# Summing the four partial sums of an adaLN gate on VectorE instead of through a copy and a 0/1 product

## The chip, the cores and the metric

The kernel runs on one core of a Trainium2 chip. The metric is the device time of one execution in microseconds, taken as the median over several runs; lower is better.

## The reference

One layer of a hybrid decoder is computed for a prompt of 1024 tokens and for 8 samples of 4 tokens each. The whole working is float32. What matters here is the condition path: nine condition rows (one of the prompt, eight of the samples) go through one linear layer whose last third is the gate of the residual.

```python
def adaln_in(x, c, w_ada, b_ada, g_norm):
    mod = jax.nn.silu(c) @ w_ada + b_ada
    shift, scale, gate = jnp.split(mod, 3, axis=-1)
    h = rmsnorm(x, g_norm) * (1 + scale[:, None, :]) + shift[:, None, :]
    return h, gate[:, None, :]

def layer(x, c, ...):
    h, gate = adaln_in(x, c, w_ada, b_ada, g_norm)
    (mq, mk, mv, mi, mf, mo, mz, aq, ak, av, az, gm, ga) = split_in(h @ w_in)
    ...
    u = jax.nn.sigmoid(gm) * (y_m @ w_mo) + jax.nn.sigmoid(ga) * (y_a @ w_ao)
    x = x + gate * (u @ w_o)
```

`c` has 9 rows of 1024, `w_ada` is 1024 x 3072, so the gate is 9 x 1024. The kernel works it out as two halves of 512 columns (`ga0`, `ga1`).

## The kernel before, in words

The program is one long run of projections on TensorE, with everything else laid beside them. After the norm and the shift and scale of the conditions (up to about 65 us) the input projections follow column block by column block: the attention's queries (`g_aq`), then the mLSTM's queries, keys and values head by head (`g_mq`, `g_mk`, `g_mv`; three pieces of 384, 384 and 288 columns each, float32 split into a high and a low part, hence three products for each), then the blocked products of the gates (`bx`, `bw`, `by`, `bz`), the output projections (`g_w_mo`), and the last rows (`foX`, `foW`, `foY`, `foZ`).

Side work is fed in between these products. It is written as Python generators, and a planner, `class Side`, decides while the program is being built where each next step of a generator stands in TensorE's order. The planner keeps a clock of its own, `now`, which each product moves on by its assumed cost (`mm`, line 254). A step says `yield lag, banks`: the next step comes at the earliest `lag` later, only at a visit (at least 1.5 after the last one that issued products) and only when the PSUM bank class that it names is free by the planner's account (`HOLD`, line 109). Streams run side by side: `a` the attention units (`unit`, line 813: loads `uqv`, `ukv`; scores `sc`; the softmax on VectorE and ScalarE; transposes `pt`; `oT`), `m` the mLSTM heads (`head`, line 1024: loads `hq`, `hk`, `hv`, `et`, `qw`; `tk`, `tv`, `S`; `U`; `n`; `ty`), `x` the sums of blocks (`sum_blocks`, line 1292, tiles `hb`), `g` the gate that is changed here.

TensorE's order is therefore written out by the planner (`in_order`, line 206). VectorE and ScalarE are tied to the program's order only before line 1892 and in the last rows; in between a scheduler orders them when the program is built, and then each engine runs its list in order. SyncE issues most of the loads and stores, in one list too. PSUM has eight banks in four classes of two; `pb` (line 187) hands out class `b`, which `pt`, `tk`, `tv`, `ty` and the gate share.

The gate itself is `ada_gate` (line 1896). For each half `j` it loads eight tiles of `w_ada` (`adar_ga`) and the bias (`gb`, nine partitions), and then runs `ada_rows` (line 346): eight products with 32 columns of weights each, of which four stand side by side in the array and write to the partitions from 0, 32, 64 and 96 of one bank, `ada_ga`. Each of these four quarters then holds a partial sum over two of the eight tiles; rows 0 to 8 of a quarter are the nine conditions. ScalarE copies the bank to `adas_ga`, and a step later a product with the constant `s9`, which has a one in row r, r+32, r+64, r+96 of column r, adds the four quarters (`gp`, 9 x 512). VectorE adds the bias, multiplies by 0.25, and five DMAs store the half (`gbD`, `gsD`); it is read again only when the output weights are prepared, some 130 us later. After the second half, `c32` is loaded anew.

Of the kernel before, what the change touches and what calls it, by code (L numbers as in the profile page):

```python
# [15 lines left out]
ALU = mybir.AluOpType  # L16
# [19 lines left out]
C_ID, C_S9, C_TRI, C_CM, C_AM, C_TS, C_CS, C_RS, C_S32, C_BM, C_S64 = 0, 128, 137, 265, 393, 649, 681, 713, 745, 777, 785  # L36
# [136 lines left out]
def body(tc, a):  # L173
    nc = tc.nc
    with ExitStack() as ctx:
# [5 lines left out]
        def pg(shape, name):  # L181
            return ps.tile(shape, F32, tag="g", bufs=2, name=name)

        def pa(shape, name):
            return ps.tile(shape, F32, tag="a", bufs=2, name=name)

        def pb(shape, name):
            return ps.tile(shape, F32, tag="b", bufs=2, name=name)

        def po(shape, name):  # L190
            return ps.tile(shape, F32, tag="o", bufs=2, name=name)

        def ht(shape, name, dt=F32):
            return sp.tile(shape, dt, tag="half", bufs=43, name=name)
# [11 lines left out]
        def in_order(ins, eng="PE"):  # L206
            i = getattr(ins, "ins", ins)
            no_sync(i, [last[eng]] if eng in last else [])
            last[eng] = i
# [15 lines left out]
        V, S, G = Ordered(nc.vector, "V"), Ordered(nc.scalar, "S"), Ordered(nc.gpsimd, "G")  # L225
# [15 lines left out]
        def dma(out, in_, late=False):  # L241
            stores(in_.tensor)
            issue(out, in_, late)
# [10 lines left out]
        def mm(out, lhsT, rhs, start, stop, share=1, more=False):  # L254
            n = int(np.prod(rhs.shape[1:]))
            side.now += max(n, 250) / 2400 if rhs.dtype == F32R else max(n * 4 // share, 128) / 2400
            side.products += 1
            in_order(nc.tensor.matmul(out, lhsT, rhs, start=start, stop=stop, skip_group_check=more))  # L258
# [48 lines left out]
        cst = cp.tile([128, C_END], F32, name="cst")  # L307
# [35 lines left out]
                dma(raws[-1], a["w_ada"][chunk, :, k])  # L343
            return raws

        def ada_rows(raws, name, mS):
            acc = pb([128, 512], f"ada_{name}")
            for k0 in (0, 4):
                for k in range(k0, k0 + 4):
                    j = 32 * (k % 4)  # L350
                    mm(acc[j:j + 32], c32[:, k], raws[k], start=(k < 4), stop=(k >= 4), share=4)
                yield 2.0, ("b" if k0 == 0 else "")
            S.copy(mS, acc)
            yield 2.5, "b"

        def ada_chunk(raws, name, done):
            mS = ht([128, 512], f"adas_{name}")
            yield from ada_rows(raws, name, mS)
            tp = pb([128, 4, 9], f"adat_{name}")
            for j in range(4):  # L360
                mm(tp[:, j], mS[:, j * 128:(j + 1) * 128], cst[:, C_S9:C_S9 + 9], start=True, stop=True)
            done(tp)
# [1458 lines left out]
        for n in order[:2]:  # L1821
# [5 lines left out]
        acc = [(pg([128, 384], "g_ak0"), po([128, 384], "g_av0")),  # L1827
               (po([128, 384], "g_ak1"), pg([128, 384], "g_av1")),
               (pa([128, 384], "g_ak2"), pa([128, 384], "g_av2"))]
        for q, kk in enumerate(two):  # L1830
# [44 lines left out]
            else:  # L1875
                pair_end(1, acc[1])
                gp = pb([128, 9, 8], "gp")
# [16 lines left out]
        gbD, gsD = dp.tile([1, D], F32, name="gbD"), dp.tile([NS, D], F32, name="gsD")  # L1894

        def ada_gate():
            s9 = cst[:, C_S9:C_S9 + 9]
            for j in range(2):
                cj = slice(j * 512, (j + 1) * 512)
                raws = []  # L1900
                for k in range(KT):
                    raws.append(ht([128, 512], f"adar_ga{j}{k}"))
                    dma(raws[-1], a["w_ada"][4 + j, :, k])
                    yield 2.0, ""
                gb = ht([128, 512], f"gb{j}")[:9]
                dma(gb, a["b_gate"][:, cj].to_broadcast((9, 512)))
                yield 5.0, "b"
                mS = ht([128, 512], f"adas_ga{j}")
                yield from ada_rows(raws, f"ga{j}", mS)
                yield 1.5, "b"  # L1910
                gp = pb([128, 512], f"gp{j}")[:9]
                mm(gp, s9, mS, start=True, stop=True)
                V.tensor_tensor(gb, gp, gb, op=ALU.add)
                V.tensor_scalar(gb, gb, 0.25, None, op0=ALU.mult)
                dma(gbD[:, cj], gb[0:1])
                for t in range(NT):
                    dma(gsD.rearrange("(b t) e -> b t e", t=NT)[:, t, cj], gb[1:9])
                yield 3.0, "b" if j == 0 else ""
            dma(c32, hD[:, :, SEQ:T])
# [64 lines left out]
        for g in range(4):  # L1984
            queries(g)
        side.add("g", ada_gate())
        side.add("s", sample_attention(), "b")
        blocks["t1"] = block(0, 1)
# [340 lines left out]
```

## Time and profile before

| what | us |
|---|---|
| median of 3 runs (845.09, 845.72, 845.74) | 845.72 |
| profiled execution, first to last instruction | 843.1 |
| TensorE (PE) busy in it | 823.9 |
| VectorE (DVE) busy | 599.2 |
| ScalarE (ACT) busy | 416.0 |

The profiled execution has no device time of its own on record; its span is 2.6 us shorter than the median of the runs, and that much is taken to lie around the span. PE and PEld are the products and the weight loads of TensorE, DVE is VectorE, ACT ScalarE, POOL GpSimd, SP SyncE; a row `L258` is line 258, the helper through which all products go. A float32 product shows as two records in the trace.

### The profile page before, as it was taken

The page shows a single profiled execution, that of the slowest core. Times are in us where ns is not written, and L with a number is a line of the kernel's source. Part 1 is how long each engine was busy: PE and PEld are TensorE (multiplying, and loading weights), DVE is VectorE, ACT ScalarE, POOL GpSimd, SP SyncE. Part 2 cuts the span into 40 slices and gives each one's busy share as a digit, 9 for nine tenths or more (in the row PEclk, how much of TensorE's full clock was granted, in tenths as well). Part 3 has the DMA queues.
Part 4 walks back from the last instruction along what each step waited for, and adds up shares of the span by engine and source line. Part 5 has one row for each costly group of instructions (what it writes and reads, how often), then busy time and mean ns, then how long its engine had stood idle before and what let it go on. Part 6 is the DMA issues. An engine that isn't in the chain of part 4 may idle for free.

```text
span 843.1 us, 15367 instructions
## 1 busy us (share of the span) xinstructions
PE 823.9 (98%) x5185; PEld 680.6 (81%) x5185; DVE 599.2 (71%) x1601; ACT 416.0 (49%) x1027; POOL 63.3 (8%) x108
## 2 busy tenths in 40 slices
PE   6999999999999999999999999999999999999996
PEld 3779999879989878888878777777777779997775
DVE  4887884556667586655766875788878998865676
ACT  5663346655655454554543534444436554334343
POOL 0120000000110000000000000000002104250000
PEclk9999999999999999999999999999999999999998
DMA  9996548337745653454656584556446586634522
GB/s 332 371 358 200 146 150 297 119 111 237 247 133 177 193 163 103 162 175 153 206 185 207 194 253 127 178 151 152 127 126 211 190 266 212 215 95 168 200 106 107
DMA packets 117859, 158.18 MB, mean 188 GB/s; under 512 B 29056, under 2 KB 64512, under 8 KB 117748
## 3 DMA queue, kind: packets, MB, share of 16 engines
q1 hardware_dynamic: 111556, 146.44, 55.1%
q10 hardware_dynamic: 4752, 6.56, 2.1%
q0 software_dynamic: 1472, 4.20, 1.3%
q8 instruction: 41, 0.67, 0.3%
q14 instruction: 38, 0.31, 0.1%
HBM read 113.41 MB, written 44.75 MB: 188 GB/s over the span
## 4 chain that ended last, share of the span: by engine, by line
PE 93%; DVE 4%; DMA 1%; issue 1%; ACT 1%; SPq 0%; DVEq 0%; ACTq 0%
PE by L258 10%; PE bx L258 10%; PE bw L258 10%; PE g_aq L258 6%; PE g_w_mo L258 6%; PE bz L258 5%; PE g_mk L258 4%; PE g_mq L258 4%; PE g_mv L258 3%; PE foW L258 3%; PE foX L258 3%; PE foY L258 2%; PE sc L258 2%; PE oT L258 2%; PE foZ L258 2%; PE smp L258 2%
## 5 line engine op out<-in xcount | busy, mean ns | idle before, releaser
L219 ACT ACTIVATE p<-p,nmx 128x256 f32<-128x256 f32 (+1 forms) x64 | 31.0, 486 | 26.6 <-DVE nmx L219 22.3
L258 PE MATMUL g_aq<-h_h,wh_aq 128*128 128x384 f32 (+1 forms) x96 | 32.4, 337 | 0.0
L258 PE MATMUL g_w_mo<-ym_l,wh_w_mo 128*128 128x384 f32 (+1 forms) x96 | 31.1, 324 | 0.0
L258 PE MATMUL g_aq<-h_l,wh_aq 128*128 128x384 f32 (+1 forms) x96 | 31.0, 323 | 0.0
L258 PE MATMUL g_w_mo<-ym_l,wl_w_mo 128*128 128x384 f32 (+1 forms) x96 | 31.0, 323 | 0.0
L258 PE MATMUL g_aq<-h_h,wl_aq 128*128 128x384 f32 (+1 forms) x96 | 31.0, 323 | 0.0
L258 PE MATMUL g_w_mo<-ym_h,wh_w_mo 128*128 128x384 f32 (+1 forms) x96 | 31.0, 323 | 0.0
L219 DVE CUSTOM_DVE_ANT_0 p<-sc,cst,sink 128x256 f32<-128x256 f32 (+1 forms) x64 | 26.1, 463 | 3.6 <-PE sc L258 3.5
L258 PE MATMUL g_mk<-h_h,wh_mk 128*128 128x384 f32 (+1 forms) x72 | 24.8, 344 | 0.0
L258 PE MATMUL g_mq<-h_h,wh_mq 128*128 128x384 f32 (+1 forms) x72 | 24.4, 339 | 0.0
L219 DVE TENSOR_TENSOR et<-et,cst 128x384 f32<-128x384 f32 (+1 forms) x12 | 6.2, 513 | 24.9 <-DMA et<-nmd 24.9
L219 ACT ACTIVATE gt<-gt 128x512 f32<-128x512 f32 (+1 forms) x17 | 10.4, 613 | 26.9 <-DVE gt L219 26.2
L258 PE MATMUL g_mk<-h_l,wh_mk 128*128 128x384 f32 (+1 forms) x72 | 23.3, 323 | 0.0
L258 PE MATMUL g_mq<-h_l,wh_mq 128*128 128x384 f32 (+1 forms) x72 | 23.3, 323 | 0.0
L258 PE MATMUL g_mk<-h_h,wl_mk 128*128 128x384 f32 (+1 forms) x72 | 23.2, 323 | 0.0
L258 PE MATMUL g_mq<-h_h,wl_mq 128*128 128x384 f32 (+1 forms) x72 | 23.2, 323 | 0.0
L219 ACT ACTIVATE et<-et,an 128x128 f32<-128x128 f32 x32 | 11.2, 394 | 23.1 <-DVE et L219 17.8
L258 PEld LDWEIGHTS g_aq<-h_h,wh_aq 128*128 128x128 f32 x96 | 18.0, 188 | 1.4 <-issue 1.2
L246 POOL DMA_DIRECT2D oD<-uqv x16 | 8.8, 553 | 134.1 <-ACT uqv L219 130.8
L219 ACT ACTIVATE p<-p,den 128x256 f32<-128x256 f32 (+1 forms) x32 | 14.7, 490 | 8.1 <-DVE den L219 7.9
L258 PEld LDWEIGHTS g_w_mo<-ym_h,wh_w_mo 128*128 128x128 f32 x96 | 18.0, 188 | 0.0
L258 PEld LDWEIGHTS g_w_mo<-ym_l,wh_w_mo 128*128 128x128 f32 x96 | 18.0, 188 | 0.0
(1969 smaller groups left out, 2851.8 us busy)
## 6 DMA issues: line engine op xcount, KB each, us to landing
hb<-hD SPq DMA_DIRECT2D x24, 256.0 KB
x<-xT SPq DMA_DIRECT2D x16, 256.0 KB
early_h<-w_ada SPq DMA_DIRECT2D x8, 512.0 KB
adar_ga<-w_ada SPq DMA_DIRECT2D x16, 256.0 KB
wr_ga<-w SPq DMA_DIRECT2D x16, 256.0 KB
wr_gm<-w SPq DMA_DIRECT2D x16, 256.0 KB
taD<-gt SPq DMA_DIRECT2D x16, 256.0 KB
tmD<-gt SPq DMA_DIRECT2D x16, 256.0 KB
```

The costliest lines, as they stand in the source:

```text
L219: ins = f(*args, **kw)
L246: ins = (eng or nc.sync).dma_start(out, in_)
L258: in_order(nc.tensor.matmul(out, lhsT, rhs, start=start, stop=stop, skip_group_check=more))
```

## The change

The copy to `adas_ga` and the product with `s9` go, and so do the two steps of the planner between them. Instead VectorE adds the four quarters of the bank one after another to the bias tile, straight from PSUM: four additions of 9 x 512 for each half, where there was one. `ada_rows` is cut in two, so that the other user of it (the shift and scale in the first 65 us) keeps its copy.

```diff
-        def ada_rows(raws, name, mS):
-            acc = pb([128, 512], f"ada_{name}")
+        def ada_products(raws, acc):
             for k0 in (0, 4):
                 for k in range(k0, k0 + 4):
                     j = 32 * (k % 4)
                     mm(acc[j:j + 32], c32[:, k], raws[k], start=(k < 4), stop=(k >= 4), share=4)
                 yield 2.0, ("b" if k0 == 0 else "")
+
+        def ada_rows(raws, name, mS):
+            acc = pb([128, 512], f"ada_{name}")
+            yield from ada_products(raws, acc)
             S.copy(mS, acc)
             yield 2.5, "b"
...
                 yield 5.0, "b"
-                mS = ht([128, 512], f"adas_ga{j}")
-                yield from ada_rows(raws, f"ga{j}", mS)
-                yield 1.5, "b"
-                gp = pb([128, 512], f"gp{j}")[:9]
-                mm(gp, s9, mS, start=True, stop=True)
-                V.tensor_tensor(gb, gp, gb, op=ALU.add)
+                acc = pb([128, 512], f"ada_ga{j}")
+                yield from ada_products(raws, acc)
+                for r in range(0, 128, 32):
+                    V.tensor_tensor(gb, acc[r:r + 9], gb, op=ALU.add)
                 V.tensor_scalar(gb, gb, 0.25, None, op0=ALU.mult)
```

More of the change, by code (lines that the diff above doesn't have):

```diff
@@ L1896, in ada_gate @@
         def ada_gate():
-            s9 = cst[:, C_S9:C_S9 + 9]
             for j in range(2):
```

## The prediction

> **What bounds the kernel now.** I read the page first, then busy time by stretches, then TensorE's waits, then the gate's own instructions, and last the order of the changed program's instructions, which holds no times.
>
> ```profile
> span 843.1 us, 15367 instructions
> PE 823.9 (98%) x5185; PEld 680.6 (81%) x5185; DVE 599.2 (71%) x1601; ACT 416.0 (49%) x1027; POOL 63.3 (8%) x108
> PE 93%; DVE 4%; DMA 1%; issue 1%; ACT 1%; SPq 0%; DVEq 0%; ACTq 0%
> ```
>
> TensorE's products fill the span and make up nearly all of the chain that ended last. By stretches (columns: stretch, total, then busy time of PE, PEld, DVE, ACT, POOL):
>
> ```profile
> 60.00:280.00 220.00, 219.99 (x1672) 195.16 (x1665) 141.18 (x503) 115.26 (x350) 13.39 (x29) 1.00 0.58 180
> 280.00:430.00 150.00, 146.53 (x914) 121.14 (x914) 98.30 (x297) 76.52 (x201) 5.93 (x17) 1.00 0.56 173
> ```
>
> From 60 to 280 us, where both halves of the gate lie, TensorE has 0.01 us of idle time; from 280 to 430 it has 3.47, and its waits there are these four (us in total, times, longest):
>
> ```profile
> PE bx L258 <- ACT gt L219: 1.2, 1, 1.2
> PE smp L258 <- ACT hv L219: 1.0, 1, 1.0
> PE by L258 <- DVE mkv L219: 0.9, 1, 0.9
> PE n L258 <- DVE C L219: 0.5, 1, 0.5
> ```
>
> So an instruction taken off TensorE in the first stretch shortens the kernel by its place in TensorE's order, unless another engine then comes late.
>
> **What is removed.** The gate's product and copy, and the VectorE work behind them:
>
> ```profile
> L258 PE MATMUL gp<-adas_ga,cst x4: 592/595/598, 183.6 to 256.6; 128*9 128x512 f32 x4
> L219 ACT COPY adas_ga<-ada_ga x2: 567/567/567, 162.0 to 251.6; 128x512 f32<-128x512 f32 x2
> L219 DVE TENSOR_TENSOR gb<-gp,gb x2: 678/678/678, 184.7 to 257.2; 9x512 f32<-9x512 f32 x2
> ```
>
> The durations of products overlap, so I price them by the starts around them:
>
> ```profile
> 182.59 0.44 PE L258 MATMUL oT<-p,ukv 128*64 128x128 f32 x4
> ...
> 183.61 1.03 PE L258 MATMUL gp<-adas_ga,cst 128*9 128x512 f32 x2
> 184.57 0.44 PE L258 MATMUL g_mq<-h_h,wh_mq 128*128 128x384 f32 x1
> 184.85 0.34 PE L258 MATMUL g_mq<-h_l,wh_mq 128*128 128x384 f32 x1
> 185.02 0.34 PE L258 MATMUL g_mq<-h_h,wl_mq 128*128 128x384 f32 x1
> ...
> 255.83 0.29 PE L258 MATMUL g_mq<-h_l,wh_mq 128*128 128x288 f32 x1
> 255.96 0.29 PE L258 MATMUL g_mq<-h_h,wl_mq 128*128 128x288 f32 x1
> 256.19 1.03 PE L258 MATMUL gp<-adas_ga,cst 128*9 128x512 f32 x2
> 257.14 0.40 PE L258 MATMUL g_mq<-h_h,wh_mq 128*128 128x288 f32 x1
> 257.38 0.29 PE L258 MATMUL g_mq<-h_l,wh_mq 128*128 128x288 f32 x1
> ```
>
> First half: 183.61 to 184.57, 0.96 us; the detour out of the projection stays, because `oT` stands there anyway. Second half: 0.95 us, and the detour goes with it. Neighbours of 288 columns start 0.13 apart (255.83 to 255.96), but 0.23 pass before `gp` and 0.24 after the first product behind it, so the way out and back costs 0.10 + 0.11 = 0.21. Together 0.96 + 0.95 + 0.21 = **2.12 us off TensorE**. ScalarE loses two copies, 1.1 us; it is half idle, and I count nothing for that.
>
> **What is added.** Three more additions on VectorE for each half, from partitions 32, 64 and 96 of PSUM onto partition 0. The trace does not show that on nine partitions; it does show the same move on 32, in the sums of the last sample rows:
>
> ```profile
> L219 DVE TENSOR_TENSOR fo8s<-fo,fo8s x6: 682/685/692, 785.1 to 809.4; 32x512 f32<-32x512 f32 x6
> L219 DVE TENSOR_TENSOR wor<-wor,gb x16: 683/686/694, 401.8 to 493.0; 128x512 f32<-128x512 f32 x16
> 257.25 0.68 DVE L219 TENSOR_TENSOR gb<-gp,gb 9x512 f32<-9x512 f32 x1 [0.64 <-PE gp L258]
> 257.96 0.42 DVE L219 TENSOR_SCALAR gb<-gb 9x512 f32<-9x512 f32 x1
> ```
>
> Bounds are 0.68 and 0.69 us; I take 0.68, the row with nine partitions. A step that needs the one before starts 0.71 after it (257.25 to 257.96), so four take 2.84 us, 2.13 more than now, 4.3 us for both halves.
>
> [...]
>
> **Is it covered in the first half?** The order up to the first gate is unchanged, so its surroundings can be read from the trace of before:
>
> ```profile
> 159.17 1.06 PE L258 MATMUL ada_ga<-adar_ga,c 128*32 128x512 f32 x8
> 159.79 0.69 DVE L219 TENSOR_TENSOR wl_mq<-wr_mq,wh_mq 128x512 fp32r<-128x512 f32 x1 [0.26 <-ACT wh_mq L219]
> 162.16 0.16 DVE L219 TENSOR_TENSOR den<-den,nmx 128x4 f32<-128x4 f32 x1 [1.68 <-ACT p L219]
> 163.47 0.69 DVE L219 COPY p<-pt 128x512 f32<-128x512 f32 x1 [0.54 <-PE pt L263]
> 168.91 1.03 PE L263 MATMUL pt<-cst,p 128*128 128x128 f32 x8
> ```
>
> The changed order puts three additions behind `wl_mq`, then `den`, then the fourth, then the copy of `pt`. VectorE is free at 160.48, the products have ended at 160.23: three additions run to about 162.6, `den` comes 0.4 late, the fourth ends near 163.5, and the copy starts at its old time. Behind that, the factor 0.25 and the softmax's reciprocal delay one unit's scaling by about 1 us; its transposes stand behind the `pt` of 168.91. The bank that the additions hold is taken next by the `pt` of 168.91, 5.4 us after the fourth. Cost: nothing. Without VectorE's gap of 1.68 us it would be up to 2.1.
>
> **What is moved.** The planner waited twice for bank class `b` between copy and product; the copy stands at 162, the product at 183.6. Both steps go, so the second half's eight loads, its bias, its products, the five stores of the first half and the reload of `c32` all come earlier. In the changed order the second half's products stand among head 1's `g_mk` instead of its `g_mv`, some 25 us earlier (an estimate from the products that lie between). On SyncE's list the five stores now precede loads of attention units:
>
> ```profile
> 162.93 0.38 SPq L246 DMA_DIRECT2D uqv<-qD  x1
> 188.95 0.24 SPq L246 DMA_DIRECT2D gbD<-gb  x1
> 189.24 1.28 SPq L246 DMA_DIRECT2D gsD<-gb  x4
> ```
>
> They must wait for the scaled half (about 164.6) and take 1.5 us, so a load issued at 162.93 is issued near 166.2. Its scores stand behind the place of the first `gp`, 183.61: covered by 17 us.
>
> Because the planner's clock now runs differently, the interleaving of units, heads and block sums is another one from 183 to about 430 us. Counting in TensorE's order, there are three fewer detours out of the large products; one is the `gp` already counted, so two more: 2 x 0.21 = **0.4 us**, with 0 and 0.4 as bounds.
>
> In the second half the additions stand behind `et` and `qw`, which wait for a DMA, and ahead of the copy of a unit's `pt`, which `oT` needs. Between that `pt` and that `oT` lie four scores, eight `oT` products, eighteen products of 288 and three of 384 columns:
>
> ```profile
> 238.30 1.13 PE L258 MATMUL sc<-ukv,uqv 64*128 64x256 f32 x8
> 239.37 0.40 PE L258 MATMUL g_mv<-h_h,wh_mv 128*128 128x288 f32 x1
> ```
>
> ```profile
> DVE et L219 <- DMA et<-nmd: 11.2, 5, 4.3
> ```
>
> That is 1.07 (238.30 to 239.37) + 1.02 (182.59 to 183.61) + 18 x 0.13 + 3 x 0.175 (184.85 to 185.02, rounded) = 5.0 us. The additions would end just as the `pt` does if VectorE is on time; the copy is 0.69, so about 4 us of lateness are covered. The waits for `et` between 183 and 300 us sum to 11.2 us in five, the longest 4.3. Cost taken: nothing.
>
> **The sum.** 843.1 - 2.12 - 0.4 = 840.6 us of span; with the 2.6 us around it, 843.2 us against the median of 845.72. That leaves TensorE's idle time as it is, at 3.47 us between 280 and 430.
>
> **The rivals.** *The gain is eaten by new waits.* The present interleaving leaves TensorE four waits of 0.5 to 1.2 us; another one may leave six or seven. Two or three more of about 0.9 us give 843.2 + 2.3 = 845.5 us. For: attention units follow closer on each other in the changed order, so the way from scores to transposes is shorter. Against: 220 us without a wait show that the planner's lags have slack, and the way from a head's `U` to its `n`, the place of the 0.5 us wait, is longer now.
>
> *Slower: VectorE's list sets the pace.* The additions, and the softmax copies behind them, queue behind `et`'s waits for DMAs. These 11.2 us are hidden today; if more than the 4 us of cover is used up, TensorE stands in front of `oT` and of the next unit's transposes. With half of the 11.2 exposed the time is 843.2 + 5.6 = 848.8 us. It turns slower than before once more than 2.5 us are exposed, and slower by over 0.2% once more than 4.2 are; all 4.3 us of additions uncovered is just that mark. For: 4.3 us for a single wait. Against: the loads of the second half have left the stretch where the tiles behind that wait are loaded.
>
> *TensorE isn't the limit.* Weight loads fill 81% of the span, and if products could close up into the remaining fifth, two fewer would change nothing: 845.7 us. Against it: neighbours start 0.13 and 0.175 us apart without a gap for 220 us. [...]
>
> *More is gained.* If the 0.5, 0.9 and 1.0 us waits of the old interleaving go too: 843.2 - 2.4 = 840.8 us.
>
> **Chances.** About 0.2%, 1.7 us, is what a measurement of this kernel can tell from no change, so faster means below 844.0 and slower above 847.4. Forecast 0.46, gain eaten 0.26, VectorE's list 0.17, TensorE not the limit 0.03, more gained 0.08. Faster: 0.46 + 0.08 = 0.54. Same: 0.26 + 0.03, less 0.01 of the eaten gain that falls beyond the mark, 0.28. Slower: 0.17 + 0.01 = 0.18. The range runs from 840.8, where more is gained, to 848.8, where half of the `et` waits are exposed; about 0.05 lie below and 0.12 above. The forecast's own range is 842.4 to 844.0.
>
> **What would show it.** Right: no `gp` from `adas_ga`; eight `gb` additions of 0.68 us; TensorE still without idle time from 60 to 280 us; its busy time lower by about 2.5 us. Wrong: waits of `pt` or `oT` on VectorE near 190 to 300 us, `gb` additions that start long after their products, or idle time in 280 to 430 well above 3.5 us. A single addition far above 0.7 us would overthrow the price.

## The result, and the profile after

| kernel | median us | lowest to highest | executions |
|---|---|---|---|
| before | 844.53 | 843.39 to 847.30 | 13 |
| changed | 842.77 | 841.73 to 845.38 | 13 |

The ratio is 0.9978, 95% interval 0.9969 to 0.9988: 1.8 us faster, where 843.2 us was forecast. Three more comparisons with the kernel before, told below, gave 0.9998 (0.9983 to 1.0013), 0.9997 (0.9985 to 1.0010) and 0.9984 (0.9971 to 0.9998). Over all 48 executions of the changed kernel the median is 843.88 us, over 105 of the kernel before 845.19, 1.3 us apart; comparison by comparison the medians differ by -1.8, +0.6, -0.1 and -1.6 us, 0.7 on average. So the gain that lasts is about 1 us, 0.1%, and two of the four comparisons show none. Single times of the changed kernel scatter more (a standard deviation of 1.7 us against 1.2). Why it scatters is what the experiments had to find.

The page of the changed kernel, from an execution of 845.38 us, the longest of its 13:

```profile
span 843.6 us, 15348 instructions
PE 823.8 (98%) x5181; PEld 681.4 (81%) x5181; DVE 607.4 (72%) x1607; ACT 417.2 (49%) x1025; POOL 62.9 (7%) x108
```

The four records of `gp` are gone (5185 to 5181), VectorE has 8.2 us more, and TensorE's busy time is hardly lower. In the run below that keeps the old order VectorE has only 4.0 more (603.2), next to the 4.3 that the additions were put at; where the rest comes from in the new order is not shown. The additions as a group (shortest, median and longest in ns, first and last start):

```profile
L219 DVE TENSOR_TENSOR gb<-ada_ga,gb x8: 672/684/693, 161.3 to 217.7; 9x512 f32<-9x512 f32 x8
```

And in VectorE's timeline (start, duration):

```profile
161.27 2.11 DVE L219 TENSOR_TENSOR gb<-ada_ga,gb 9x512 f32<-9x512 f32 x3
163.31 0.14 DVE L219 TENSOR_TENSOR den<-den,nmx 128x4 f32<-128x4 f32 x1
163.48 0.69 DVE L219 TENSOR_TENSOR gb<-ada_ga,gb 9x512 f32<-9x512 f32 x1
164.33 0.69 DVE L219 COPY p<-pt 128x512 f32<-128x512 f32 x1 [0.16 <-PE pt L263]
215.52 2.84 DVE L219 TENSOR_TENSOR gb<-ada_ga,gb 9x512 f32<-9x512 f32 x4
```

Eight additions at 684 ns, 2.84 us for a half, three ahead of `den` and the fourth behind it: as forecast. Now the busy time by stretches (columns as in the prediction: PE, PEld, DVE, ACT, POOL, then the granted clock), first the last stretch of the kernel before, then the three of the changed one:

```profile
430.00:750.00 320.00, 319.32 (x1851) 259.87 (x1850) 255.87 (x558) 147.08 (x318) 31.43 (x42) 1.00 0.58 179
```

```profile
60.00:280.00 220.00, 219.55 (x1682) 196.39 (x1682) 147.22 (x517) 117.21 (x355) 12.67 (x30) 1.00 0.59 186
280.00:430.00 150.00, 147.40 (x910) 122.19 (x909) 100.74 (x294) 76.72 (x197) 5.58 (x16) 0.99 0.54 170
430.00:750.00 320.00, 318.45 (x1847) 258.95 (x1846) 256.17 (x555) 146.72 (x317) 31.61 (x41) 1.00 0.56 177
```

Two things stand in these rows. Behind 430 us, where nothing was changed, TensorE's idle time has grown from 0.68 to 1.55 us. And from 280 to 430 the granted clock is 0.99, not 1.00. TensorE's waits of the changed kernel (in total, times, longest) lead to the place:

```profile
PE S L258 <- DVE C L219: 2.0, 1, 2.0
PE bw L258 <- ACT bw L219: 0.9, 1, 0.9
PE ty L263 <- ACT hv L219: 0.6, 1, 0.6
PE smp L258 <- ACT hv L219: 0.4, 1, 0.4
```

The waits `bx` 1.2, `smp` 1.0, `by` 0.9 and `n` 0.5 of the old interleaving are gone or smaller, and a wait of 2.0 us is new: `S`, an mLSTM head's scores, waits for `C`, the head's state, which VectorE updates. VectorE's timeline, and the row of TensorE that waited:

```profile
403.37 0.69 DVE L219 TENSOR_TENSOR wor<-wor,gb 128x512 f32<-128x512 f32 x1 [1.26 <-DMA wor<-w_out]
403.98 0.34 DVE L219 SCALAR_TENSOR_TENSOR C<-C,dec,U 128x129 f32<-128x129 f32 x1
404.38 1.12 PE L258 MATMUL S<-hq,hk 128*128 128x128 f32 x6 [1.97 <-DVE C L219]
```

`C` stands on VectorE's list directly behind a product that scales a tile of the output weights (`wor`, in `out_weights`), and that one waits for its load. Then the clock, by stretches of 1 us (the last column but two):

```profile
403.00:404.00 1.00, 0.00 (x0) 0.00 (x0) 0.63 (x2) 0.65 (x3) 0.10 (x1) 1.00 0.89 317
405.00:406.00 1.00, 1.00 (x5) 0.90 (x5) 0.93 (x4) 0.90 (x3) 0.00 (x0) 0.50 0.88 311
407.00:408.00 1.00, 1.00 (x4) 0.80 (x3) 0.83 (x6) 0.01 (x1) 0.00 (x0) 0.50 0.21 52
408.00:409.00 1.00, 1.00 (x6) 0.82 (x5) 0.93 (x4) 0.00 (x0) 0.00 (x0) 0.80 0.00 0
```

After the wait TensorE's clock is halved, from 405 to 408.4 us. 3.4 us at half speed lose 1.7 us, and TensorE shows as fully busy all the while. So this execution paid 2.0 + 1.7 = 3.7 us at one place that the prediction does not mention.

### The profile page after: what moved, and what is told of

Same layout as the page of the kernel before. It is cut to its first block, busy times and chain, and to the rows that moved or that the text cites. A ratio compares the mean times of both kernels' runs of the same rounds, so it can differ in the third digit from the quotient of the medians.

```text
span 843.6 us, 15348 instructions
## 1 busy us (share of the span) xinstructions
PE 823.8 (98%) x5181; PEld 681.4 (81%) x5181; DVE 607.4 (72%) x1607; ACT 417.2 (49%) x1025; POOL 62.9 (7%) x108
## 4 chain that ended last, share of the span: by engine, by line
PE 91%; DMA 4%; DVE 3%; ACT 1%; issue 1%; SPq 0%; DVEq 0%; ACTq 0%
PE by L258 10%; PE bx L258 10%; PE bw L258 9%; PE g_aq L258 6%; PE g_w_mo L258 6%; PE bz L258 5%; PE g_mq L258 4%; PE g_mk L258 4%; PE g_mv L258 3%; PE foW L258 3%; PE foX L258 3%; PE foY L258 2%; PE sc L258 2%; PE oT L258 2%; PE foZ L258 2%; PE smp L258 2%
## 5 line engine op out<-in xcount | busy, mean ns | idle before, releaser
L258 PEld LDWEIGHTS g_aq<-h_l,wh_aq 128*128 128x128 f32 x96 | 18.1, 188 | 0.0
L258 PEld LDWEIGHTS g_aq<-h_h,wl_aq 128*128 128x128 f32 x96 | 18.0, 188 | 0.0
L258 PEld LDWEIGHTS g_w_mo<-ym_l,wl_w_mo 128*128 128x128 f32 x96 | 18.0, 188 | 0.0
```

## The experiments

Each run is set against runs of the kernel before on the same chip.

**The changed kernel again** (no edit).

> The changed kernel unchanged, as the reference of the other three on the same chip and for a second profile. Theory (the two products with the constant were 2.1 us of TensorE's time, and TensorE sets the pace): about 2.0 us under the kernel before, TensorE's busy time 2 to 2.5 us lower than before's 823.9. Rival (the new interleaving brings the gain, the products were worth little): the same total, which the next two runs divide.

Measured: 846.20 us (841.82 to 847.72), ratio 0.9998 (0.9983 to 1.0013). Its waits:

```profile
PE S L258 <- DVE C L219: 2.7, 1, 2.7
PE bw L258 <- ACT bw L219: 2.3, 2, 1.2
```

The same two waits, longer: 5.0 us where the first profile had 2.9, and the same halved clock behind the first of them. The gain of the first comparison was not there, and TensorE's busy time is 823.2 us, 0.7 below that of before and not 2 to 2.5.

**The new order with the products put back** (one product with `s9` in each half, which the planner does not count).

```diff
                 acc = pb([128, 512], f"ada_ga{j}")
+                in_order(nc.tensor.matmul(acc[:9], cst[:, C_S9:C_S9 + 9], raws[0], start=True, stop=True))
                 yield from ada_products(raws, acc)
```

> The changed kernel with one product with the constant put back on TensorE for each half, right ahead of the first product of the half and into the same bank, where the next product overwrites it; its result is not used. The planner's clock does not see it, so TensorE's order is that of the changed kernel but for these two. Theory: 2 x 0.96 = 1.9 us slower than the changed kernel, so about the kernel before, within 0.5 us; the interleaving alone is worth 0.4 us or nothing. Rival (the interleaving brings the gain): as fast as the changed kernel, within 0.5 us. Rival (TensorE has room): the same, within 0.5 us.

Measured: 846.05 us, ratio 1.0011 (0.9996 to 1.0027). Against the kernel before, the new interleaving alone brings no gain; its wait of `S` was 2.5 us here, with the halved clock behind it. But the changed kernel of the same batch stood at 846.20, so the 1.9 us that were forecast between the two don't show: with standard deviations of 1.9 and 2.0 us among their executions, these medians can't decide it. TensorE's starts can. Here with the product put back, and then the same place in the changed kernel:

```profile
152.17 0.59 PE L1911 MATMUL ada_ga<-adar_ga,cst 128*9 128x512 f32 x1
153.98 0.44 PE L258 MATMUL g_mk<-h_h,wh_mk 128*128 128x384 f32 x1
```

```profile
153.19 0.60 PE L258 MATMUL ada_ga<-adar_ga,c 128*32 128x512 f32 x1
154.20 0.44 PE L258 MATMUL g_mk<-h_h,wh_mk 128*128 128x384 f32 x1
```

The stretch is 1.81 us instead of 1.01, so the product costs 0.80 there, and 0.83 in the second half (1.82 instead of 0.99). That is less than the 0.96 of `gp`: its two records start 0.43 apart, among those of the gate's own products.

**The additions in the old order** (TensorE's order of before less the two products).

```diff
                     V.tensor_tensor(gb, acc[r:r + 9], gb, op=ALU.add)
+                yield 2.5, "b"
+                yield 1.5, "b"
+                side.now += 512 * 4 / 2400
+                side.products += 1
```

> The additions of the changed kernel, but after them the two steps of the planner are kept and its clock is moved on as the product moved it, so that TensorE's order is that of the kernel before, less the two products. Theory: 1.9 to 2.1 us faster than the kernel before, so the same as the changed kernel within 0.5 us, with the four waits of before (0.5, 0.9, 1.0, 1.2 us) still there. Rival (the interleaving brings the gain): within 0.5 us of the kernel before. Rival (VectorE's list sets the pace): slower than before, by the 4.3 us of added additions at the most.

Measured: 843.78 us (842.63 to 845.51), ratio 0.9983 (0.9973 to 0.9994). Its waits are three of the old ones and one at `tv` in the place of `n`, none above 1.2 us, and its clock is 1.00 up to the end of TensorE's work:

```profile
PE smp L258 <- ACT hv L219: 1.2, 1, 1.2
PE by L258 <- DVE mkv L219: 1.1, 1, 1.1
PE bx L258 <- ACT gt L219: 1.1, 1, 1.1
PE tv L263 <- issue: 1.0, 1, 1.0
```

1.8 us faster than before with nothing off TensorE's list but the two products: they are worth about what the prediction took, and the additions cost nothing that shows.

**Four more additions in each half** (they cancel out).

```diff
                     V.tensor_tensor(gb, acc[r:r + 9], gb, op=ALU.add)
+                for op in (ALU.add, ALU.subtract) * 2:
+                    V.tensor_tensor(gb, gb, acc[0:9], op=op)
```

> The changed kernel with the VectorE work behind the products doubled: after the four additions of a half, quarter 0 is added and taken off twice more (four operations of 0.68 us, 0.71 apart, 2.8 us for each half), ahead of the release of the bank. Theory (VectorE's additions lie under TensorE's work): the first half costs nothing, since about 5 us lie between the additions and the next use of the bank; the second half stands in front of a copy that the attention output waits for, with some cover left, so between 0 and 2.8 us slower than the changed kernel, 1.5 us at the likeliest. Rival (VectorE's list sets the pace already): the full 5.7 us slower.

Measured: 843.47 us, ratio 0.9980 (0.9968 to 0.9991). Doubling the additions made nothing slower; the 1.5 us taken as likeliest did not come. That it came out ahead of the unedited kernel beside it goes with a shorter wait of `S`, behind which the clock was not halved:

```profile
PE S L258 <- DVE C L219: 1.4, 1, 1.4
```

**The output weights on GpSimd** (so that no load stands in front of `C`; TensorE's order as in the changed kernel).

```diff
-                    V.tensor_tensor(t, t, gb[f], op=ALU.mult)
+                    G.tensor_tensor(t, t, gb[f], op=ALU.mult)
...
-                    V.tensor_tensor(b22, b22, b12, op=ALU.subtract)
+                    G.tensor_tensor(b22, b22, b12, op=ALU.subtract)
...
```

> The changed kernel with one edit: the 16 products and 8 sums that scale the output weights (wor<-wor,gb and wor<-wor,wor) run on GpSimd instead of VectorE; TensorE's order is that of the changed kernel, instruction for instruction. Theory: in the changed order the state update C stands on VectorE's list behind a product of the output weights that waits for its load (1.26 us at 402 us), and TensorE waits 2.0 to 2.7 us for C in front of S; and the copy of bw waits, through gt, behind a difference of output weights that waits 4.03 us for a store. With the output weights on another list both waits go (S behind C 0, bw behind ScalarE 0), and the time is 2.0 + 0.9 us (first profile) to 2.7 + 2.3 us (second one) below the changed kernel in the same batch, with less spread: about 841 us, all runs below 844. Rival: C is late for another reason (U, or VectorE's own load): the wait in front of S stays at 1.4 to 2.7 us and the time is that of the changed kernel. Second rival: GpSimd's products slow VectorE or the stores come too late for the reload of the weights: slower than the changed kernel by 1 us or more.

Measured: 851.68 us, ratio 1.0083 (1.0052 to 1.0115). The wait of `S` is gone, as the theory had it; the second rival came true all the same. GpSimd's work, and VectorE's beside it:

```profile
447.78 6.38 POOL L219 TENSOR_TENSOR wor<-wor,gb 128x512 f32<-128x512 f32 x4 [11.93 <-DMA wor<-w_out]
451.34 1.67 DVE L219 TENSOR_TENSOR wr_ga<-ws,wr_ga 128x512 f32<-128x512 f32 x1
452.94 0.67 DVE L219 TENSOR_TENSOR gt<-p,by 128x512 f32<-128x512 f32 x1
456.43 6.06 POOL L219 TENSOR_TENSOR wor<-wor,wor 128x512 f32<-128x512 f32 x4 [1.74 <-DMA woDb<-wor]
458.75 0.89 DVE L219 TENSOR_TENSOR ws<-wr_gm,wr_gm 128x512 f32<-128x512 f32 x1 [4.04 <-DMA wr_gm<-w]
459.56 1.78 DVE L219 TENSOR_TENSOR wl_pgate__5650<-wr_ga,wh_pgate__5649 128x512 fp32r<-128x512 f32 x1
```

While GpSimd adds or multiplies, VectorE's additions with two operands in SBUF take up to 1.78 us (0.89, 1.67 and 1.78 in these rows) instead of 0.69; `gt`, whose second operand is in PSUM, takes 0.67 here and 0.685 on average in the kernel before. That the place of its operand is what spares `gt` is not shown by this one row. The wait of `bw` was not cured either: `gt` stands behind `ws` as well, which waits 4.04 us for a load of weights. That half of the theory fell. TensorE's timeline has waits of three lengths:

```profile
420.42 0.30 PE L258 MATMUL smp<-wr_ga,c 128*32 128x128 f32 x2 [1.84 <-ACT gts L219]
441.24 0.51 PE L258 MATMUL bw<-t2h,wh_pgate__5410 128*128 128x512 f32 x1 [1.66 <-ACT bw L219]
467.15 0.79 PE L258 MATMUL bw<-t2h,wh_pgate__5649 128*128 128x512 f32 x1 [3.21 <-ACT bw L219]
```

And the granted clock in a stretch of 1 us after each:

```profile
422.00:423.00 1.00, 1.00 (x4) 0.71 (x4) 1.00 (x2) 0.00 (x0) 1.00 (x1) 0.50 0.00 0
442.00:443.00 1.00, 1.00 (x8) 0.88 (x8) 0.69 (x2) 1.00 (x3) 0.00 (x0) 1.00 0.67 178
468.00:469.00 1.00, 1.00 (x3) 0.74 (x3) 0.78 (x2) 1.00 (x3) 0.00 (x0) 0.50 0.61 152
```

A wait of 1.84 us is followed by the halved clock, one of 1.66 is not, one of 3.21 is.

**The same in the old order** (the edit above in the kernel with TensorE's old order).

> The control for the run above: the same move of the output weights to GpSimd, in the kernel with the new additions and TensorE's old order less its two products (843.78 us before, no wait in front of S). Theory: there the output weights stand in front of nothing that TensorE needs soon, so the move brings nothing: 843.8 us within 0.8, and the waits smp 1.2, by 1.1, bx 1.1 stay. Rival (fewer VectorE instructions help everywhere, or GpSimd slows something): a change of 2 us or more here as well.

Measured: 852.27 us, ratio 1.0091 (1.0076 to 1.0106). The theory expected no effect and missed by 8.5 us. The move costs about the same in either order, so these two runs say nothing on the price of the wait in front of `S`. In both profiles it shows on TensorE as waits of `bw` (5.1 and 6.0 us in all) and the halved clock behind the long ones; how much of that is the slower additions and how much later loads is not shown.

**Eight products more** (the kernel before, its `gp` issued five times in each half).

```diff
                 mm(gp, s9, mS, start=True, stop=True)
+                for _ in range(4):
+                    in_order(nc.tensor.matmul(gp, s9, mS, start=True, stop=True))
```

> The kernel before, with its 0/1 product of the gate issued five times instead of once in each half, eight more in all, the planner's clock left alone, so that the rest of TensorE's order is that of before. Theory (TensorE's list sets the time, each product is worth its place, 0.95 to 0.96 us): 8 x 0.95 = 7.6 us slower than before, with bounds of 6.4 (if products behind each other start closer together) and 7.7 us. Rival (TensorE is not the limit, weight loads are): no change, within 1 us. Rival (VectorE's additions behind it become late): above 8.5 us.

Measured: 853.99 us, ratio 1.0105 (1.0089 to 1.0121), 9.1 us slower. TensorE's starts in the first half:

```profile
183.41 1.03 PE L258 MATMUL gp<-adas_ga,cst 128*9 128x512 f32 x2
184.27 3.60 PE L1914 MATMUL gp<-adas_ga,cst 128*9 128x512 f32 x8
187.80 0.44 PE L258 MATMUL g_mq<-h_h,wh_mq 128*128 128x384 f32 x1
435.63 0.50 PE L258 MATMUL bx<-h_h,wh_pgate__5267 128*128 128x512 f32 x1 [2.31 <-ACT gt L219]
```

183.41 to 187.80 is 4.39 us; less the 0.96 of the one product of before, four products take 3.43, 0.86 each, 6.9 for eight. The rest is waits and clock: `bx` waits 2.3 us here instead of 1.2 and then has the halved clock. In sum the waits are 0.8 longer and the clock costs 1.7. The time passed the forecast's upper bound of 7.7 us, which had no room for either; the rival above 8.5 us has the size, but no wait for `gb` shows. That TensorE is not the limit is refuted: what is put on its list is paid.

**The changed kernel a third time** (no edit).

> The changed kernel once more, beside the others of this batch. The first measurement gave 842.77 us (ratio 0.9978), the second 846.2 (0.9998). Theory: the difference is in the waits behind transfers that the new order has (S behind C 1.4 to 2.7 us, bw 0.9 to 2.3 us), which vary from run to run and chip to chip; so a median anywhere between 842.7 and 846.3, single runs spread over 5 us, the longer runs with more of these waits. Rival: the second measurement was a chance draw, median within 0.5 us of 842.8.

Measured: 844.74 us (842.96 to 846.99), ratio 0.9997 (0.9985 to 1.0010). Its profile has a shorter wait of `S` in TensorE's timeline, 1.10 us:

```profile
402.33 0.94 PE L258 MATMUL S<-hq,hk 128*128 128x128 f32 x6 [1.10 <-DVE C L219]
```

and the clock behind it stayed at 1.00:

```profile
403.00:404.00 1.00, 1.00 (x7) 0.85 (x6) 0.90 (x6) 0.97 (x4) 0.00 (x0) 1.00 0.85 297
```

Its `bw` waited 2.6 us in two parts, the longer 1.3.

**`C` first** (an ordering edge on VectorE's list, and nothing else; TensorE's order as in the changed kernel).

```diff
...
+                        newest["C"] = V.scalar_tensor_tensor(Cn, chain[-1], ...)
...
+        def after_c(ins):
+            no_sync(getattr(ins, "ins", ins), [getattr(newest["C"], "ins", newest["C"])])
...
-                    V.tensor_tensor(t, t, gb[f], op=ALU.mult)
+                    after_c(V.tensor_tensor(t, t, gb[f], op=ALU.mult))
```

> The changed kernel with one edit of order: the products that scale the output weights (wor<-wor,gb) are put behind the newest state update C on VectorE's list, by an ordering edge and nothing else; TensorE's order is that of the changed kernel, instruction for instruction. Theory: the wait of TensorE for C near 404 us is a wait behind the load of an output-weight tile, and where it lasts about 2 us or more (1.97, 2.46 and 2.68 in three profiles) TensorE's granted clock falls to 0.50 for about 3.4 us behind it, which costs another 1.7; where it lasts 1.1 or 1.4 us the clock stays at 1.00. With C first the wait in front of S is gone and no stretch of 2 us has a clock below 0.98 before 838 us: 1.1 to 1.4 us below the shortest and up to 4.4 us below the longest executions of the changed kernel, so about 2.5 us below its median in this batch, near 841.8 us, with the slow executions (above 845) gone. Rival: the wait moves on to bw or gt, whose product queues behind the same output weights: bw waits longer by as much as S waits less, and the time is that of the changed kernel within 0.7 us.

Measured: 840.98 us (840.64 to 843.08), ratio 0.9957 (0.9941 to 0.9973), against 843.66 for the changed kernel beside it. VectorE's timeline, TensorE's row and the waits:

```profile
400.38 0.35 DVE L219 SCALAR_TENSOR_TENSOR C<-C,dec,U 128x129 f32<-128x129 f32 x1 [0.83 <-PE n L258]
400.65 1.28 DVE L219 TENSOR_TENSOR wor<-wor,gb 128x512 f32<-128x512 f32 x2
401.28 0.83 PE L258 MATMUL S<-hq,hk 128*128 128x128 f32 x6
```

```profile
PE smp L258 <- ACT gts L219: 1.1, 1, 1.1
PE bw L258 <- ACT bw L219: 1.0, 1, 1.0
PE ty L263 <- ACT hv L219: 0.6, 1, 0.6
```

`S` no longer waits; where the fourth profile below has a wait of `S` of 2.2 us, a wait of `smp` of 1.1 stands here instead. Nothing above 1.1 us is left behind 60 us, and the clock stays at 1.00 up to the end of TensorE's work. This is the version that beats both kernels.

**Twelve more additions in each half** (`* 6` in the place of `* 2` above; they cancel out).

> The changed kernel with twelve more additions and subtractions of the first partial sum in each half (they cancel out), chained behind the four: 12 x 0.71 = 8.5 us more of VectorE in each half, 17 in all, TensorE's order unchanged. Theory of the prediction: the first half has 5.4 us of cover before pt takes the bank, the second about 4 us before a unit's copy is needed; so 3.1 and 4.5 us come out, if they stand in one chain ahead of the softmax work: 7.6 us slower than the changed kernel, with waits of pt or oT for VectorE between 165 and 225 us. Rival: the additions are dealt out between the softmax instructions and only the bank is held longer: at most the 3.1 us of the first half, and less where the other bank of the class is free: 0 to 3 us slower. Second rival: all is hidden, within 1 us.

Measured: 848.04 us, ratio 1.0034 (1.0020 to 1.0049), 4.4 us above the changed kernel beside it. One wait is new, with the halved clock behind it:

```profile
230.43 0.67 DVE L219 TENSOR_TENSOR gb<-gb,ada_ga 9x512 f32<-9x512 f32 x1
231.16 0.90 PE L263 MATMUL tv<-cst,hv 128*128 128x128 f32 x3 [2.52 <-DVE gb L219]
```

2.5 + 1.7 = 4.2 us, close to the 4.4 of the medians; the forecast of 7.6 and the rival's 0 to 3 both missed. It is the second half's bank, held until the last addition; VectorE dealt the additions out between the softmax work, and neither `pt` nor `oT` waited. In the first half the additions ran to 174 us and TensorE waited for nothing.

**The changed kernel a fourth time** (no edit).

> The changed kernel once more, beside the run with C first. Theory: executions fall into two kinds, by whether the wait in front of S is below or above some 1.7 us: with the clock at 1.00 throughout about 842 to 844 us, with it at 0.50 for 3.4 us about 844.5 to 847; the median depends on how many fall to each side. The profile shows one of the two: a wait of 1.1 to 1.4 us and no low stretch near 405 us, or a wait of 2 us or more and a low stretch. Rival: the clock has nothing to do with that wait: a low stretch without a wait above 1.7 us, or a wait above 2 us without one.

Measured: 843.66 us (842.30 to 848.47), ratio 0.9984 (0.9971 to 0.9998). The profile shows the long kind, a wait of 2.22 us with the halved clock behind it; its time of 844.22 is above the median. That the executions fall into two clear groups isn't shown: the single times run on without a gap.

**The control: `C` first in the kernel before.**

> The control for the run with C first: the same ordering edge (the products that scale the output weights behind the newest C on VectorE's list) put into the kernel before, whose TensorE order stays as it was. There no wait in front of S stands in the profile. Theory: the edge is worth something only in the order that the change brings, so the time is that of before within 0.8 us, with the waits by, bx and smp of 0.9 to 1.2 us still there. Rival: the edge helps by itself, whatever the order: 2.5 us or more below before.

Measured: 845.15 us, ratio 0.9995 (0.9982 to 1.0008). The edge is worth nothing that shows in the old order; what it saves is the new order's own wait.

**The profiles on one account** (without the two with GpSimd). The start of an execution varies: the last four products of the gate's first half stand at 158.5 to 160.6 us. So the account begins there. From the span behind that point I take off the waits that TensorE's list of waits shows behind it, and the loss to the clock (the sum of 1 minus the granted clock over stretches of 1 us); what is left is TensorE's own work, with the 7 us behind its last product.

| kernel | span behind the first products | waits | clock | left |
|---|---|---|---|---|
| before | 683.9 | 4.2 | 0 | 679.7 |
| before, `C` first | 685.3 | 5.4 | 0 | 679.9 |
| before, eight products more | 693.2 | 5.0 | 1.7 | 686.5 |
| changed, first profile | 683.6 | 4.5 | 1.7 | 677.4 |
| changed, second | 686.0 | 6.7 | 1.7 | 677.6 |
| changed, third | 683.7 | 5.6 | 0 | 678.1 |
| changed, fourth | 684.0 | 5.0 | 1.7 | 677.3 |
| four more additions | 682.2 | 4.4 | 0 | 677.8 |
| twelve more additions | 687.4 | 6.6 | 3.4 | 677.4 |
| `C` first | 680.9 | 3.8 | 0 | 677.1 |
| additions in the old order | 683.2 | 5.2 | 0 | 678.0 |
| products put back | 685.1 | 5.1 | 1.7 | 678.3 |

In the new order the change takes 1.6 to 2.6 us of work off TensorE, 2.2 on average, and in the old order 1.7; the waits with what they do to the clock decide how much of that is seen. The rows of one program differ by up to 0.8, so the 0.4 us of the two other detours can't be told apart here. The last row holds only one of its two products: the other stands at 152.17, before the account begins. So it should lie 0.83 above the changed kernel (677.6 on average) and lies 0.7 above.

The record also has the mean granted clock of each execution. Ten of the 48 executions of the changed kernel have 0.996 or less, and they took 846.2 us on average, the other 38 843.7; of the kernel before, one of 92 has so little, and with `C` first none of 6. So part of the scatter goes with the clock, but the 38 still scatter by 1.4 us, and which waits the executions without a profile had is not shown.

## Why the prediction was right, and where it was not

- **What bounds the kernel, and the price of the products: right.** 2.12 us for the products and their detour and 0.4 for the two other detours were forecast; the account shows 1.6 to 2.6, 2.2 on average, in the new order, and 1.7 in the old one, whose median is 1.8 lower. The 0.4 by itself is not shown. A single product behind another is 0.86 us, a little less than the 0.96 that stand between it and a neighbour of another kind.
- **The additions: right.** 684 ns each, 2.84 us for a half, no extra cost for a read of PSUM on other partitions: an addition out of PSUM took 684 ns beside the 686 of `wor` out of SBUF, and eight reads in each half cost no time that shows (843.47 us). Sixteen cost 4.4 us, through the bank that they held.
- **The cover in the first half: right in the result, wrong in a step.** The load behind the stores was put at 166.2 us and stands at 167.06, in an execution whose products stand 0.87 later. But the `pt` of 168.91 does not take the bank next: additions up to 174 us held nothing up.
- **The cover in the second half: right in the result, wrong in the place.** The additions did not queue behind long waits of `et`: they ran in one piece at 215.52. What would have become late first was not the copy of `pt` but the bank, for `tv`.
- **The moved second half: right.** Its products stand 27 us earlier (241.56 to 214.31; 25 were estimated).
- **TensorE's idle time left as it is: the step that failed.** The prediction watched 280 to 430 us and kept 3.47 us there; 2.60 were left in the first profile. It did not look at VectorE's list behind the gate, where the shifted interleaving set a product that waits for a load in front of `C`. This new wait is of the kind of the first rival, new waits in the place of the old ones, at 1.1 to 2.7 us for `S` and 0.9 to 2.6 for `bw`; it takes back up to all of the gain, and lasts differently in each profile. The rival had priced waits at their length; each one of about 2 us cost 1.7 more.
- **The time around the span: mis-sized.** The 2.6 us compared one execution's span with other executions' median. Times and spans of the same execution differ by 1.8 us (845.38 and 843.6). With that the forecast would have been 842.4, close to the first median and 1.5 below that of all executions: the term that was too large stood in for the waits that were left out. That the forecast of 843.2 lies near the median of all executions, 843.88, is in part luck.
- **What would show it.** No `gp` and eight additions of 0.68 came true. TensorE was not without idle time from 60 to 280 (0.45 us, a wait of `smp` for `hv`), and its busy time fell by only 0.1 in the first profile: a halved clock counts as busy, and where the clock stayed up it fell by 2.2 (823.9 to 821.7).

## What to carry to other kernels

Where TensorE is the limit, a step taken off its list was worth about its place (2.12 us by the starts, 1.7 off TensorE's work in the old order), and the price could be read from the starts around it. But a change that shifts a planner's clock reorders everything behind it: look on the other engines' lists for an instruction that waits for a transfer and stands in front of one that TensorE needs, and take it out of the way by an ordering edge. And look at the granted clock behind each wait of TensorE: here every wait of 1.84 us or more came with a stretch at half speed, which cost about 1.7 us on top of its length.

## What the runs showed of the hardware

- A wait of TensorE of 1.84 us or more (1.84, 1.97, 2.01, 2.22, 2.31, 2.46, 2.52, 2.68, 3.21 and 3.54 in eight profiles) came each time with a stretch at a granted clock of 0.50. It was 3.41 us long, a loss of 1.7 us, and once, at the wait of 3.21, 6.83. It began between 1.0 us before the end of the wait and 1.4 us after it. No wait of up to 1.66 us had one; where between 1.66 and 1.84 the mark lies, and whether it is always the same, is not shown. The 6 to 7 us ahead of the program's first product are an exception: the record has 1.00 behind them.
- VectorE's additions of two SBUF tiles took up to 1.78 us instead of 0.69 beside GpSimd's, and with 24 such instructions moved there the kernel was 0.8 to 0.9% slower than before.
